# Out-projection order and low parts of the attention outputs in a two-layer hybrid encoder

## The chip, the cores and the metric

The kernel runs on one core of a Trainium2 chip. The metric is the device time of one execution in microseconds, as the median of several. An execution is a single launch that computes the whole output from the weights in HBM. The engines are named as the profile names them: PE is TensorE (matmuls), PEld its weight loads, DVE is VectorE, ACT ScalarE, POOL GpSimd, SP the engine that issues most DMAs.

## The reference, cut to what matters

A sequence of 512 tokens of width 1024 passes two layers. A layer is half a SwiGLU feed-forward block, a mixer, and another half block. The mixer projects the normalised input once and splits the columns among four groups of heads, each 256 wide:

```python
h = rms_norm(x, mix_norm)
aq, ak, av, bu, cq, ck, cv, dq, dk, dv = split(h @ w_in)
o_a = banded_attention(...)      # A: window +-128, sink, 4 query heads on 2 key heads
y_b = s5_bidirectional(bu, ...)  # B: state-space scan, then a half GLU
o_c = dilated_attention(...)     # C: three dilations, 4 heads
o_d = neighborhood_attention(...)# D: 2-D windows with a learned bias, 4 heads
x = x + concat([o_a, y_b, o_c, o_d]) @ w_out
```

All of it is in float32. The out-projection is a sum over the four groups, so its parts can be added to `x` in any order once the group is there.

## The kernel before

Activations lie transposed: `x` is eight tiles of 128 channels by 512 tokens. Every float32 product is made of three matmuls in a faster format: each operand is split into a rounded high part and the rest, the low part, and `mm3` (L107) multiplies the weights' low part with the activations' high part (L108), then high with low (L109), then high with high (L110). For the weights of layer 0's mixer ScalarE makes the high part (L126) and GpSimd the low one (L127); those of layer 1 were split ahead of time during layer 0's second feed-forward block, stored to DRAM, and are loaded as `wh` and `wl` by SP (L167, L168). There are four buffers for each of the two.

The mixer is a set of streams cut into steps, and the table `ORDER` (L35) says in which order the steps are written. `dq`, `dk`, `dv` and their like are projections. `Ds` is the first half of a step of D's attention (`first`, L736): scores, bias, exponentials, and GpSimd's division by the sum. `Dt` is the second (`second`, L769): transposing the probabilities, splitting them (L787 ScalarE high, L788 VectorE low) and multiplying by the values into `pot`. `A` and `C` are alike. Two heads share a tile `m` and then a split tile `mt` [128 x 2 x 512]: ScalarE copies half of `pot` to `tmp` (L796), VectorE adds the other half (L805, L801 for D), ScalarE writes the high part of `mt` (L808), and the low part follows on L809. S5 makes its own two `mt` (L958, L959). `mD`, `mB`, `mC` and `mA` are steps of the out-projection (`merge`, L814): D's pairs, S5's, C's two pairs together with A's first pair, and A's second pair. Each takes weights from `split`, sums in a bank of the tag `mm` (three banks), and VectorE adds the bank to `x` (L831).

The written order is a priority. A scheduler with its own estimate of durations orders each engine's instructions, so a step may be spread among others; at run time each engine goes through its list in order and waits on semaphores.

Of the kernel before, what the change touches and what calls it, by code (L numbers as in the profile page):

```python
# [15 lines left out]
ALU = mybir.AluOpType  # L16
# [18 lines left out]
ORDER = """  # L35
dq dq dq dk dk dq dq dk s5 dk dv cq dk s5 Ds dv dv ck cq ck Ds cq dv Ds dv Ds Ds s5 cq s5 Dt ck s5 Dt s5 Dt ck
cq s5 Ds cv Dt aq cv s5 aq Ds Dt Dt Ds ck Cs cv Dt s5 cv aq ak aq Cs s5 ak Dt Cs aq Cs Ct ak mD ak Cs Ct Cs Cs
Ct ak Cs Ct s5 mD Ct mD As Ct As Ct Ct As mD As As At As As mB At As At At At mC mC mB mB mC At At mC At mC mC
mC mB mC mA mA
"""  # L40
T2 = 15
# [30 lines left out]
def hybrid_encoder(ctx: ExitStack, tc: tile.TileContext, t: dict):  # L72
# [4 lines left out]
    tt = nc.vector.tensor_tensor  # L77
# [3 lines left out]
    gtt = nc.gpsimd.tensor_tensor  # L81
# [6 lines left out]
    def t2(name="t", dt=F32):  # L88
        return pool.tile([P, S], dt, tag="t2", bufs=T2, name=nm(name))

    def k4(shape, dt=F32, name="k"):
        return pool.tile(shape, dt, tag="k4", bufs=K4, name=nm(name))
# [7 lines left out]
    def bank(tag, name=None):  # L100
        bufs = {"mm": 3, "ot": 1, "sc": 2, "tp": 2}[tag]
        return ps.tile([P, 512], F32, tag=tag, bufs=bufs, name=nm("p" + (name or tag)))

    def f32(ap):
        return ap.bitcast(F32)
# [455 lines left out]
    def mixer(l, T, next_norm):  # L561
# [171 lines left out]
        def attention(res, qk, vs, band, biases, perm, is_a):  # L733
# [35 lines left out]
            def second(i, part):  # L769
                rows = slice(64 * (i % 2), 64 * (i % 2) + 64)  # L770
                vh = i % 2 if is_a else i
                v = vs[0]
                if part == 0:
                    live["ot"] = bank("ot", name="ot")
                pq = live[i]
                ot = live["ot"]
                order = (0, 3, 1, 2) if band else (0, 1, 2, 3)
                for kb in order[2 * part:2 * part + 2]:
                    qbs = [b for b in range(4) if pq[b][1] <= kb < pq[b][2]]
                    q0, q1 = qbs[0] * P, (qbs[-1] + 1) * P  # L780
                    n = q1 - q0
                    tp = bank("tp", name="tp")
                    for b in qbs:
                        c0 = (kb - pq[b][1]) * P
                        nc.tensor.transpose(tp[:, b * P - q0:(b + 1) * P - q0], pq[b][0][:, c0:c0 + P], ident)  # L785
                    pT = k4([P, 2, S], F32R, name="pT")
                    nc.scalar.copy(pT[:, 0, :n], tp[:, :n])  # L787
                    tt(pT[:, 1, :n], tp[:, :n], f32(pT[:, 0, :n]), op=ALU.subtract)  # L788
                    first = kb == 0
                    nc.tensor.matmul(ot[:, q0:q1], v[:, kb, vh, :], pT[:, 0, :n], start=first, stop=False)  # L790
                    nc.tensor.matmul(ot[:, q0:q1], v[:, kb, vh, :], pT[:, 1, :n], start=False, stop=kb == order[-1])  # L791
                if part == 0:
                    return
                live.pop(i)
                tmp = t2(name="tmp")
                nc.scalar.copy(tmp[0:64], ot[64:128])  # L796
                if i % 2 == 0:
                    live["m"] = t2(name="m")
                m = live["m"]
                if perm:  # L800
                    tt(m[rows].rearrange("p (r b c) -> p b r c", r=8, b=4),  # L801
                       ot[0:64].rearrange("p (b r c) -> p b r c", r=8, b=4),
                       tmp[0:64].rearrange("p (b r c) -> p b r c", r=8, b=4), op=ALU.add)
                else:
                    tt(m[rows], ot[0:64], tmp[0:64], op=ALU.add)  # L805
                if i % 2 == 1:
                    mt = k4([P, 2, S], F32R, name="mt")
                    nc.scalar.copy(mt[:, 0], m)  # L808
                    gtt(mt[:, 1], m, f32(mt[:, 0]), op=ALU.subtract)  # L809
                    res[i // 2].append(mt)  # L810

            return first, second
# [325 lines left out]
```

## Time and profile before

| | |
|---|---|
| median of three runs | 1983.24 us (1981.26 to 1988.75) |
| profiled execution | 1987.2 us, of it span 1985.4 |
| busy in the span | PE 1938.4, PEld 1634.4, DVE 1244.2, ACT 801.5, POOL 294.5 |
| mean granted clock of TensorE | 0.994 |

Times in the rows below are us from the start of the span. Layer 0's mixer ends near 640, layer 1's near 1635. A timeline row gives the start, the time that the instruction took, engine, line and tiles, and in brackets how long the engine was idle before it and what ended that. Matmuls overlap, so the distance between two starts is what one costs. A PEclk of 1.00 is 2.4 GHz, 0.50 is 1.2 GHz.

### The profile page before, as it was taken

The numbers are of one execution on the slowest core, as the hardware profiler recorded it, in microseconds if no ns is written. First come the engines' busy times: TensorE is split into PE (matmuls) and PEld (weight loads), VectorE is DVE, ScalarE is ACT, GpSimd is POOL, SyncE is SP. The second block draws the span as 40 slices with busy tenths as digits, with TensorE's granted clock in tenths as the row PEclk, the third lists the DMA queues.
The fourth block names the chain that finished last, engine by engine and source line by source line (L and its number), as shares of the span: only waits on it lengthen the run. The fifth ranks groups of instructions, "written<-read, shape, count | busy, mean of one in ns | idle before, by whom it ended". The sixth has DMA issues, their size and how long they took to land. (4 is left out here: it accounts for less than half of the span.)

```text
span 1985.4 us, 26849 instructions
## 1 busy us (share of the span) xinstructions
PE 1938.4 (98%) x9667; PEld 1634.4 (82%) x9667; DVE 1244.2 (63%) x2439; ACT 801.5 (40%) x1515; POOL 294.5 (15%) x403
## 2 busy tenths in 40 slices
PE   9999999999999999999999999899999999999999
PEld 7778878899977888888887888788998778888887
DVE  6976637748787554545677755475587865454454
ACT  5333323524675433333443333333346643232332
POOL 2121201112353010101022112000122310000000
PEclk9999999999999999999999999999999999999999
DMA  5444446564412362636455453544535223323233
GB/s 180 146 161 153 169 113 206 197 217 127 136 56 91 95 228 91 228 106 212 157 173 165 146 173 114 155 137 146 179 115 165 75 93 99 104 88 104 86 107 105
DMA packets 120229, 277.65 MB, mean 140 GB/s; under 512 B 24208, under 2 KB 33168, under 8 KB 120096
## 3 DMA queue, kind: packets, MB, share of 16 engines
q1 hardware_dynamic: 106496, 231.82, 38.3%
q0 software_dynamic: 13600, 44.12, 5.8%
q8 instruction: 76, 1.25, 0.3%
q14 instruction: 57, 0.47, 0.1%
HBM read 226.93 MB, written 48.99 MB: 139 GB/s over the span
## 5 line engine op out<-in xcount | busy, mean ns | idle before, releaser
L126 ACT CAST wh<-wr 128x512 fp32r<-128x512 f32 (+2 forms) x628 | 349.3, 564 | 758.8 <-PE pgp L110 264.8
L127 DVE TENSOR_TENSOR wl<-wr,wh 128x512 fp32r<-128x512 f32 (+2 forms) x610 | 390.7, 644 | 304.7 <-ACT wh L126 302.6
L108 PE MATMUL pop<-a,wl 128*128 128x512 f32 x704 | 275.3, 394 | 15.8 <-DVE wl L127 13.2
L108 PE MATMUL pgp<-hh,wl 128*128 128x512 f32 x704 | 274.3, 390 | 2.5 <-DVE wl L127 1.5
L108 PE MATMUL pup<-hh,wl 128*128 128x512 f32 x704 | 275.0, 391 | 0.4 <-DVE wl L127 0.4
L109 PE MATMUL pop<-a,wh 128*128 128x512 f32 x704 | 274.7, 390 | 0.0
L110 PE MATMUL pop<-a,wh 128*128 128x512 f32 x704 | 274.7, 390 | 0.0
L109 PE MATMUL pup<-hl,wh 128*128 128x512 f32 x704 | 274.5, 390 | 0.0
L109 PE MATMUL pgp<-hl,wh 128*128 128x512 f32 x704 | 274.2, 390 | 0.3 <-DVE hl L241 0.3
L110 PE MATMUL pup<-hh,wh 128*128 128x512 f32 x704 | 274.1, 389 | 0.0
L110 PE MATMUL pgp<-hh,wh 128*128 128x512 f32 x704 | 274.1, 389 | 0.0
L108 PEld LDWEIGHTS pop<-a,wl 128*128 128x128 f32 x704 | 132.5, 188 | 47.9 <-DVE wl L127 16.6
L108 PEld LDWEIGHTS pgp<-hh,wl 128*128 128x128 f32 x704 | 132.2, 188 | 31.3 <-DVE wl L127 2.3
L108 PEld LDWEIGHTS pup<-hh,wl 128*128 128x128 f32 x704 | 132.1, 188 | 28.7 <-DVE wl L127 0.8
L110 PEld LDWEIGHTS pop<-a,wh 128*128 128x128 f32 x704 | 132.5, 188 | 28.1
L109 PEld LDWEIGHTS pgp<-hl,wh 128*128 128x128 f32 x704 | 132.1, 188 | 27.9 <-DVE hl L241 0.6
L110 PEld LDWEIGHTS pup<-hh,wh 128*128 128x128 f32 x704 | 132.2, 188 | 27.5
L109 PEld LDWEIGHTS pup<-hl,wh 128*128 128x128 f32 x704 | 132.2, 188 | 27.4
L109 PEld LDWEIGHTS pop<-a,wh 128*128 128x128 f32 x704 | 132.6, 188 | 26.8
L110 PEld LDWEIGHTS pgp<-hh,wh 128*128 128x128 f32 x704 | 132.1, 188 | 27.3
L152 POOL DMA_DIRECT2D pd<-phi x86 | 47.0, 546 | 625.2 <-ACT phi L149 619.7
L108 PE MATMUL ppr<-wh,hl 128*128 128x256 f32 x448 | 129.5, 291 | 0.7 <-DMA wh<-pd 0.7
(275 smaller groups left out, 3054.3 us busy)
## 6 DMA issues: line engine op xcount, KB each, us to landing
wr<-in_f_w SPq DMA_DIRECT2D x172, 512.0 KB, 3.5
wr<-in_f_w SPq DMA_DIRECT2D x64, 384.0 KB, 3.3
wr<-in_f_w SPq DMA_DIRECT2D x64, 320.0 KB, 2.9
pd<-phi POOLq DMA_DIRECT2D x78, 256.0 KB, 3.9
pd<-plo POOLq DMA_DIRECT2D x78, 256.0 KB, 4.5
wl<-pd SPq DMA_DIRECT2D x78, 256.0 KB, 2.8
wh<-pd SPq DMA_DIRECT2D x78, 256.0 KB, 3.1
praw<-in_wm SPq DMA_DIRECT2D x68, 256.0 KB, 4.7
```

Of the source, the lines that this page charges most:

```text
L108: nc.tensor.matmul(out, ll, rh, start=start, stop=False)
L109: nc.tensor.matmul(out, lh, rl, start=False, stop=False)
L110: nc.tensor.matmul(out, lh, rh, start=False, stop=stop)
L126: nc.scalar.copy(hi[:, :w], r)
L127: (nc.gpsimd if pooled else nc.vector).tensor_tensor(lo[:, :w], r, f32(hi[:, :w]), op=ALU.subtract)
L152: nc.gpsimd.dma_start(dst[0], f32(hi[:, :step]))
```

## The change

Two edits. In the table one line differs (the new line is a permutation of the old): the first `mB` stands one A step later, the second and third stand ahead of the three `mC` that they followed, between A's steps; the last `mB` stays. And the low part of every attention `mt` is subtracted by VectorE (`tt`), not GpSimd (`gtt`).

```diff
-Ct ak Cs Ct s5 mD Ct mD As Ct As Ct Ct As mD As As At As As mB At As At At At mC mC mB mB mC At At mC At mC mC
+Ct ak Cs Ct s5 mD Ct mD As Ct As Ct Ct As mD As As At As As At mB As At At mB At mB mC mC mC At At mC At mC mC
 mC mB mC mA mA
...
                     nc.scalar.copy(mt[:, 0], m)
-                    gtt(mt[:, 1], m, f32(mt[:, 0]), op=ALU.subtract)
+                    tt(mt[:, 1], m, f32(mt[:, 0]), op=ALU.subtract)
```

L809 is issued twelve times, six in a layer. The scheduler orders anew what the table moves; both layers come out alike. Three places are shown, all of layer 0. In the names, `pop` are out-projection banks; their sources are `mt_5642` and `mt_5656` (S5), `mt_5628` and `mt_5826` (C's pairs), `mt_6056` (A's first pair) and `mt_6242` (A's second).

TensorE while A's heads begin, before: `ptp` are transposes of probabilities, `pot_5782` is C's last head, `p_5729` to `p_5771` belong to A's first head.

```order
L791 MATMUL pot_5782<-pT_5808,v_5084 128x512
L790 MATMUL pot_5782<-pT_5818,v_5084 128x512
L785 MATMUL ptp_5898<-ident,p_5729 128x128
L791 MATMUL pot_5782<-pT_5818,v_5084 128x512
L785 MATMUL ptp_5898<-ident,p_5735 128x128
L108 MATMUL pop_6142<-mt_5642,wl_6079 128x512
L109 MATMUL pop_6142<-mt_5642,wh_6078 128x512
L110 MATMUL pop_6142<-mt_5642,wh_6078 128x512
L108 MATMUL pop_6142<-mt_5656,wl_6079 128x512
L785 MATMUL ptp_5906<-ident,p_5765 128x128
L109 MATMUL pop_6142<-mt_5656,wh_6078 128x512
L110 MATMUL pop_6142<-mt_5656,wh_6078 128x512
```

The same transposes in the new order (`psc` are scores, 5833 to 5867 of A's second head, 5885 of its third):

```order
L790 MATMUL pot_5782<-pT_5808,v_5084 128x512
L791 MATMUL pot_5782<-pT_5808,v_5084 128x512
L785 MATMUL ptp_5898<-ident,p_5729 128x128
L790 MATMUL pot_5782<-pT_5818,v_5084 128x512
L785 MATMUL ptp_5898<-ident,p_5735 128x128
L791 MATMUL pot_5782<-pT_5818,v_5084 128x512
L785 MATMUL ptp_5906<-ident,p_5765 128x128
L785 MATMUL ptp_5906<-ident,p_5771 128x128
L749 MATMUL psc_5861<-o_5578,o_5304 128x384
L750 MATMUL psc_5861<-kl_5579,o_5304 128x384
L749 MATMUL psc_5867<-o_5578,o_5304 128x256
L750 MATMUL psc_5867<-kl_5579,o_5304 128x256
```

S5's products 6134 and 6142, which stood among these transposes, now stand further ahead. From `psc_5833` to the first product with `mt_6056` there are 24 out-projection matmuls in the old order and 9 in the new.

TensorE at the end of the mixer, before; `pot_6193` is A's last head, and after the last row ten more fillers follow up to the first product with `mt_6242`:

```order
L108 MATMUL pop_6298<-mt_5656,wl_6083 128x512
L109 MATMUL pop_6298<-mt_5656,wh_6082 128x512
L790 MATMUL pot_6193<-pT_6234,v_5441 128x384
L110 MATMUL pop_6298<-mt_5656,wh_6082 128x512
L791 MATMUL pot_6193<-pT_6234,v_5441 128x384
L108 MATMUL pop_6306<-mt_5642,wl_6083 128x512
L109 MATMUL pop_6306<-mt_5642,wh_6082 128x512
L110 MATMUL pop_6306<-mt_5642,wh_6082 128x512
L108 MATMUL pop_6306<-mt_5656,wl_6083 128x512
L109 MATMUL pop_6306<-mt_5656,wh_6082 128x512
```

The new order there:

```order
L109 MATMUL pop_6314<-mt_6056,wh_6251 128x512
L110 MATMUL pop_6314<-mt_6056,wh_6251 128x512
L790 MATMUL pot_6193<-pT_6225,v_5441 128x384
L791 MATMUL pot_6193<-pT_6225,v_5441 128x384
L790 MATMUL pot_6193<-pT_6234,v_5441 128x384
L791 MATMUL pot_6193<-pT_6234,v_5441 128x384
L108 MATMUL pop_6325<-mt_6242,wl_6280 128x512
L108 MATMUL pop_6335<-mt_6242,wl_6280 128x512
L108 MATMUL pop_6344<-mt_6242,wl_6280 128x512
```

In the old order fifteen matmuls stand between the last `pot_6193` and the first with `mt_6242`, in the new one none.

VectorE where S5's `mt` are split, before; `mb` are S5's unsplit outputs, `ISA` rows on L752 add the bias and take the minimum:

```order
L752 ISA p_5729,mn_5724<-psc_5726,bias_5722 128x256
L752 ISA mn_5724 128x1
L752 ISA p_5735,mn_5724<-psc_5732,bias_5722 128x384
L752 ISA mn_5724 128x1
L959 SCALAR_TENSOR_TENSOR mt_5642<-mb_5640,mt_5642 128x512
L959 SCALAR_TENSOR_TENSOR mt_5656<-mb_5654,mt_5656 128x512
L788 TENSOR_TENSOR pT_5681<-ptp_5676,pT_5681 128x512
```

And in the new order:

```order
L752 ISA p_5729,mn_5724<-psc_5726,bias_5722 128x256
L752 ISA mn_5724 128x1
L752 ISA p_5735,mn_5724<-psc_5732,bias_5722 128x384
L752 ISA mn_5724 128x1
L809 TENSOR_TENSOR mt_5628<-m_5517,mt_5628 128x512
L959 SCALAR_TENSOR_TENSOR mt_5642<-mb_5640,mt_5642 128x512
L959 SCALAR_TENSOR_TENSOR mt_5656<-mb_5654,mt_5656 128x512
L788 TENSOR_TENSOR pT_5681<-ptp_5676,pT_5681 128x512
```

The low part of C's first pair, which GpSimd subtracted, now stands in front of S5's two, and S5's products are summed into banks 71 to 73 in a row (71 and 72 before). On SP, layer 1 loads the second block of S5's weights ahead of C's first block; in the old order it was the other way round. GpSimd's list only loses L809 and has its weight subtractions in the new order of blocks.

## Rows read from the trace of the kernel before

**Rows 1.** The page, part 1: busy us (share of the span), instructions.

```profile
PE 1938.4 (98%) x9667; PEld 1634.4 (82%) x9667; DVE 1244.2 (63%) x2439; ACT 801.5 (40%) x1515; POOL 294.5 (15%) x403
```

**Rows 2.** Waits of TensorE, 560 to 640: us in total, times, longest.

```profile
PE pop L108 <- ACT mt L808: 1.8, 1, 1.8
PE pop L108 <- ACT mt L958: 1.5, 1, 1.5
```

**Rows 3.** Waits of TensorE, 1550 to 1625 (layer 1).

```profile
PE pop L109 <- DMA wh<-pd: 1.9, 1, 1.9
...
PE pop L108 <- ACT mt L958: 1.4, 1, 1.4
PE pop L108 <- DMA wl<-pd: 0.7, 1, 0.7
```

**Rows 4.** Timeline, 605 to 608, then layer 1: start, us, instruction [idle before].

```profile
605.25 0.42 PE L791 MATMUL pot<-pT,v 128*128 128x384 f32 x1
...
605.71 0.58 ACT L796 COPY tmp<-pot 64x512 f32<-64x512 f32 x1 [0.33 <-PE pot L791]
...
606.33 0.68 DVE L805 TENSOR_TENSOR m<-pot,tmp 64x512 f32<-64x512 f32 x1 [0.47 <-ACT tmp L796]
607.04 0.62 ACT L808 CAST mt<-m 128x512 fp32r<-128x512 f32 x1 [0.75 <-DVE m L805]
...
607.71 0.73 PE L108 MATMUL pop<-mt,wl 128*128 128x512 f32 x2 [1.82 <-ACT mt L808]
...
1592.09 1.64 PE L108 MATMUL pop<-mt,wl 128*128 128x512 f32 x3 [1.82 <-ACT mt L808]
```

**Rows 5.** Timeline at the end of the mixer, layer 0: TensorE, then ScalarE.

```profile
625.12 0.33 PE L791 MATMUL pot<-pT,v 128*128 128x384 f32 x1
625.29 0.40 PE L108 MATMUL pop<-mt,wl 128*128 128x512 f32 x1
...
628.74 0.61 PE L108 MATMUL pop<-mt,wl 128*128 128x512 f32 x2
...
627.41 0.62 ACT L808 CAST mt<-m 128x512 fp32r<-128x512 f32 x1
```

**Rows 6.** Groups by line and form: busy us, mean ns of one.

```profile
L788 DVE TENSOR_TENSOR pT<-ptp,pT 128x512 fp32r<-128x512 f32 x32 | 21.4, 681 | 4.7 <-ACT pT L787 4.6
...
L809 POOL TENSOR_TENSOR mt<-m,mt 128x512 fp32r<-128x512 f32 x12 | 15.4, 1287 | 39.7 <-ACT mt L808 39.7
```

**Rows 7.** Timeline near 575: TensorE, VectorE, GpSimd; VectorE in layer 1.

```profile
575.49 0.79 PE L109 MATMUL pop<-mt,wh 128*128 128x512 f32 x1 [0.20 <-POOL mt L809]
...
574.55 2.85 DVE L959 SCALAR_TENSOR_TENSOR mt<-mb,mt 128x512 fp32r<-128x512 f32 x2
...
574.16 1.28 POOL L809 TENSOR_TENSOR mt<-m,mt 128x512 fp32r<-128x512 f32 x1
...
1557.99 2.07 DVE L959 SCALAR_TENSOR_TENSOR mt<-mb,mt 128x512 fp32r<-128x512 f32 x2
```

**Rows 8.** Timeline of TensorE: nine matmuls from the first row to the second.

```profile
581.40 0.48 PE L108 MATMUL pop<-mt,wl 128*128 128x512 f32 x1
...
583.58 0.39 PE L790 MATMUL pot<-pT,v 128*128 128x512 f32 x1
```

**Rows 9.** Windows: length, busy us by engine (instructions), PEclk, DMA share, GB/s.

```profile
587.89:605.89 18.00, 17.30 (x98) 14.00 (x96) 14.70 (x48) 14.49 (x47) 9.51 (x15) 1.00 0.28 79
1574.20:1590.30 16.10, 14.41 (x82) 11.52 (x80) 12.00 (x43) 12.24 (x39) 6.37 (x11) 1.00 0.12 37
609.10:612.50 3.40, 3.40 (x13) 2.92 (x12) 1.74 (x4) 1.80 (x4) 0.81 (x2) 0.50 0.02 5
...
1600.50:1603.90 3.40, 3.40 (x15) 2.79 (x16) 0.69 (x1) 0.00 (x0) 0.00 (x0) 1.00 0.16 51
```

**Rows 10.** Timeline of the DMA issues on SP, layer 1.

```profile
1592.90 1.27 SPq L168 DMA_DIRECT2D wl<-pd  x3
1596.26 1.27 SPq L167 DMA_DIRECT2D wh<-pd  x3
```

## The prediction

> **What bounds the kernel now.** I read the page first: TensorE is busy for 1938.4 of 1985.4 us [rows 1], so time can only move where TensorE waits or runs at a lower clock. Then the waits of TensorE in the two mixer tails, which is where the change moves anything. In layer 0 there are two long ones: 1.5 us on S5's `mt` (call it wait 1) and 1.8 us on the `mt` of A's first pair (wait 2) [rows 2]. Layer 1 has the same two (1.4 us, and wait 2 again with 1.82 us) and two waits for weights, 1.9 and 0.7 us [rows 3, 4]. Everything else in the tails is dense. So even a perfect reordering could win only these, some 9 us, and what the clock loses behind them.
>
> Wait 2 is a fixed latency: the last `pot` matmul starts at 605.25 and ends at 605.67, ScalarE copies half of it, VectorE adds, ScalarE casts, and TensorE starts at 607.71 [rows 4]. From the end of that matmul to the first one that needs `mt` it is 2.04 us, whatever else happens. At the end of the mixer the same chain stands for A's second pair, but there TensorE has work: its last `pot` starts at 625.12, fifteen other matmuls follow from 625.29, and when TensorE comes to `mt` at 628.74 it has been ready since 628.03 [rows 5]. That covered chain and the stretch in front of wait 2 are what I look at in the change.
>
> **The change part by part.** All sums are against the profiled execution (1987.2 us, span 1985.4), which is 4.0 us above the median of 1983.24; I add the difference to the median.
>
> *Waits 1 and 2 themselves: 0.* In the new order the matmuls in front of both, and those that wait, stand at the same places; only which product is computed differs.
>
> *Low parts on VectorE, behind wait 1: +0.4 us a layer.* One such operation costs VectorE about 0.68 us (I take the `pT` subtraction, 681 ns, also 128x512) where GpSimd needed 1.287 [rows 6]. Where the low part of `mt` is waited for, that would be a gain of 0.6 us, but the trace has only one such wait on TensorE, 0.20 us at 575.49 [rows 7]. Behind wait 1 the new operation (C's first `mt`) is queued in front of the two L959 operations, whose results the very next TensorE matmuls now need; the C matmuls that stood between them are gone. L959 thus ends one operation later, TensorE waits about 0.6 instead of 0.2. Bounds 0 and 0.7; I take 0.4 more. The other low parts: those of D and of C's second pair have other matmuls between high and low part, and at wait 2 three L108 matmuls and a `pot` (0.8 us) cover 0.7. Nothing, at most one operation each.
>
> On L959 itself the trace shows 2.85 us for the two in layer 0, where GpSimd subtracts a low part beside them from 574.16, and 2.07 us in layer 1 [rows 7]. The Trainium skill says in "SBUF — State Buffer", Who interferes with whom, that a VectorE instruction with two SBUF inputs contends with a GpSimd instruction that reads SBUF; the trace agrees, 2.85 against 2.07. By that page the moved operation, which has two SBUF inputs itself, would be held up beside GpSimd as L959 was, this term would stand at its upper bound, 0.7 a layer, and the sum at +9.3.
>
> *S5 tokens earlier: +2.4 us a layer in front of wait 2.* In the old order 24 out-projection matmuls stand between the scores `psc_5833` of A's second head and wait 2, in the new one 9: fifteen S5 and C matmuls have moved ahead of that stretch. At 0.24 us each (nine from 581.40 to 583.58 take 2.18 [rows 8]) they are 3.6 us, of which I count 3.5, since the first after a transpose costs more. Ahead of the stretch there was no idle time for them to fill, so the stretch starts about 3.5 us later, and must end as early as before for the sum to be zero. Lower bound 0: A's work has slack. Upper bound 3.5: A's heads set the pace and every matmul taken away leaves a hole. Nearest row: in 18.0 us of this stretch in layer 0 VectorE is busy 14.7, ScalarE 14.5, and TensorE already idles 0.7 with the cover in place; in layer 1 it idles 1.7 of 16.1 [rows 9]. Taking away 3.5 leaves 14.5 us. VectorE has then three `x` additions less and one low part more (14.7 - 2 x 0.68 = 13.3), ScalarE about the same 14.5 less one weight cast. Engines that hand tiles to each other in order don't run at 95 to 100%, so I take 2.4, nearer the upper end.
>
> *The end of the mixer: +2.1 us a layer.* In the new order the last four `pot` matmuls stand behind all fillers, and the matmul after them is the first that needs A's second `mt`. The cover of fifteen matmuls is gone and wait 2's 2.04 us stands here too, call it wait 3. I count 2.0 to 2.7 (VectorE has a weight subtraction in front of the addition, 0.7) and take 2.1. This is the surest term, since it follows from the order of one engine.
>
> *Weights of layer 1: -1.1 us.* The wait of 0.7 on `wl` was for a block that is now loaded while S5's products run, so it goes. The one of 1.9 comes because three `wh` loads can't start until 1596.26, when the matmuls that hold the buffers are through, though the `wl` loads were issued at 1592.90 [rows 10]. Now those matmuls come two to three us sooner after wait 2, but TensorE also comes sooner to the block it needs: I take -0.4 (bounds -1.9 and +1).
>
> *Clock: 0.* Behind waits 1 and 2 the granted clock is at 0.5, the level of 1.2 GHz: 609.10 to 612.50 has 0.50 with TensorE busy throughout, so each such stretch costs up to 3.4/2 = 1.7 us. But the 1.9 us wait for `wh` left the clock at 1.00 [rows 9]. So a wait of this size may or may not cost 1.7. Of five, four did. With wait 3 there are two more chances, and the four old ones can fall either way: sum 0, bounds -6.8 and +3.4.
>
> The Trainium skill, in "TensorE: Matmul & The Clock Gate", What's actually happening, says that the gate is free-running and its effect "run-variable". The trace agrees: waits of 1.8 and 1.9 us ended differently. By that rule alone the four old losses might be absent in a new execution, which is the rival of the clock below.
>
> Sum: 2 x (0.4 + 2.4 + 2.1) - 1.1 + 0 = +8.7. Against the median: 1983.24 + 8.7 = 1992 us; the profiled execution would be near 1996.
>
> **Rivals.**
> 1. *Only wait 3.* A's heads have slack after all, the moved matmuls cost nothing in front of wait 2: 2 x 2.1 + 0.8 - 1.1 = +3.9, 1987. For it: VectorE and ScalarE each have a fifth of that stretch free. Against: TensorE idles there even with the cover.
> 2. *Slower beyond doubt.* A's heads set the pace fully (3.5 a layer) and wait 3 lowers the clock in both layers (1.7 each): 2 x (0.4 + 3.5 + 2.1 + 1.7) - 1.1 = +14.3, 1997.5. For it: wait 2, built the same, did so in both layers. Against: `wh` at 1.9 us did not. It decides from about 2.9 a layer in front of wait 2, or from one lowered clock more than before.
> 3. *Faster, by the clock.* The four stretches at half clock in the tails don't come: 4 x 1.7 = 6.8 less. With rival 1's small loss that is 3.9 - 6.8 = -2.9, 1980. For it: the clock spared the `wh` wait. Against: waits 1 and 2 stay as long as they are, and in both layers they lowered it. Even this doesn't reach half a per cent.
> 4. *Nothing happens.* The queues run as before and the moved work is the same work: 0, 1983. Against it wait 3, which follows from TensorE's own order.
>
> **How the numbers follow.** Half a per cent, 9.9 us, is about what a measurement of this kernel can tell from no change. Forecast 50% (its own range +5.5 to +12.5, the sizes of the two middle terms), rival 1 20%, rival 2 20%, rival 3 6%, rival 4 4%. The forecast lies just inside the bound: of its 50% some 24 are above +9.9, with all of rival 2 that makes slower 0.44; faster by half a per cent is left 0.03, for what I have not seen; the rest, 0.53, within. For 8 in 10 I leave out rivals 3 and 4 and the upper third of rival 2, 17% together: 1985 to 2000.
>
> **What would show it.** In the new trace: a wait on `mt` L808 of about 2 us at the last `pot` of each mixer, which is not there now; if it is absent, the forecast falls. From the scores `psc` of A's second head to wait 2 TensorE should idle 2 to 4 us in pieces below 1.5, on `pT` and on `mn`, where it idled 0.7 in layer 0; if less than 1, rival 1. Waits 1 and 2 should keep their 1.4 to 1.8 us; if either is gone, my reading of the order is wrong. The wait for `wl` in layer 1 should be gone and that for `wh` be 1 to 2 us. The low parts should show as VectorE operations of 0.6 to 0.7 us, longer beside GpSimd. The granted clock behind waits 1, 2 and 3 decides between forecast, rival 2 and rival 3.

## The result, and the profile after

The changed kernel takes 2000.68 us (median of eight runs, 1993.07 to 2003.67). The kernel before, run beside it and with the three runs shown earlier, has a median of 1987.78 over eight. The ratio is 1.0068, 95% interval 1.0050 to 1.0086: slower, by 12.9 us of medians. The forecast was 1992 with a range of 1985 to 2000, so the time lies just outside it, on the slow side. Two things, of nearly equal size, make up the 8.7 us between forecast and result: the median of before that I added to stood 4.5 us lower than that of more runs, and the change itself cost 4.2 us more than the sum of +8.7.

The profiled execution of the changed kernel took 2003.67 us (span 2001.9, mean granted clock 0.991). Its page, part 1, against [rows 1]:

```profile
PE 1946.6 (97%) x9667; PEld 1640.1 (82%) x9667; DVE 1251.2 (63%) x2451; ACT 801.9 (40%) x1515; POOL 278.2 (14%) x391
```

TensorE's count is the same and its busy time is 8.2 us longer, which, with the same instructions, fits more time at the lower clock. VectorE has the twelve low parts more, GpSimd twelve less. Waits of TensorE in layer 0, 560 to 650, against [rows 2] (total, times, longest):

```profile
PE pop L108 <- ACT mt L808: 4.0, 2, 2.3
PE pop L108 <- ACT mt L958: 1.6, 1, 1.6
PE psc L749 <- DVE mn L752: 1.4, 2, 1.2
PE pot L790 <- DVE m L805: 1.2, 1, 1.2
PE pop L109 <- DVE mt L959: 1.1, 1, 1.1
PE pot L791 <- DVE pT L788: 0.5, 1, 0.5
```

There are now two waits on L808: wait 2 is still there and wait 3 stands beside it. Four rows of 0.5 to 1.4 us follow, where before had nothing above 0.5. In layer 1, against [rows 3], the 0.7 on `wl` is gone and the wait for `wh` is 1.8:

```profile
PE pop L108 <- ACT mt L808: 3.7, 2, 2.1
...
PE pop L109 <- DMA wh<-pd: 1.8, 1, 1.8
```

The end of the mixer in layer 0, all engines (start, us, instruction, idle before), against [rows 5]:

```profile
634.24 0.33 PE L791 MATMUL pot<-pT,v 128*128 128x384 f32 x1
634.61 0.58 ACT L796 COPY tmp<-pot 64x512 f32<-64x512 f32 x1
634.62 0.69 DVE L127 TENSOR_TENSOR wl<-wr,wh 128x512 fp32r<-128x512 f32 x1
635.34 0.68 DVE L805 TENSOR_TENSOR m<-pot,tmp 64x512 f32<-64x512 f32 x1
636.06 0.62 ACT L808 CAST mt<-m 128x512 fp32r<-128x512 f32 x1 [0.87 <-DVE m L805]
...
636.82 1.07 PE L108 MATMUL pop<-mt,wl 128*128 128x512 f32 x2 [2.25 <-ACT mt L808]
```

This is wait 3, link by link: copy, a weight subtraction that stands in front of the addition, addition, cast. The fifteen matmuls that lay over it are gone, and TensorE is idle for 2.25 us.

In front of wait 2, TensorE, against [rows 4] and [rows 9]:

```profile
599.43 0.39 PE L749 MATMUL psc<-o,o 128*128 128x256 f32 x1 [1.17 <-DVE mn L752]
...
608.47 0.38 PE L790 MATMUL pot<-pT,v 128*128 128x256 f32 x1 [1.16 <-DVE m L805]
...
609.62 0.58 PE L791 MATMUL pot<-pT,v 128*128 128x256 f32 x1 [0.54 <-DVE pT L788]
...
615.05 0.97 PE L108 MATMUL pop<-mt,wl 128*128 128x512 f32 x3 [1.73 <-ACT mt L808]
```

Windows of the changed kernel (busy us by engine, then the granted clock): the 20.62 us up to the end of wait 2, then 3.4 us inside that stretch, behind wait 2, and behind wait 3:

```profile
594.43:615.05 20.62, 15.73 (x81) 12.19 (x80) 13.65 (x47) 14.10 (x43) 8.20 (x16) 0.92 0.20 62
609.40:612.80 3.40, 3.18 (x10) 2.44 (x11) 1.52 (x5) 1.38 (x6) 1.83 (x4) 0.54 0.45 135
615.20:618.60 3.40, 3.40 (x20) 2.99 (x21) 3.07 (x6) 2.39 (x7) 1.37 (x2) 1.00 0.02 5
636.90:640.30 3.40, 3.40 (x9) 2.62 (x10) 1.43 (x3) 0.36 (x1) 0.00 (x0) 0.51 0.31 125
```

The same length up to wait 2 in the kernel before:

```profile
587.09:607.71 20.62, 18.11 (x103) 14.69 (x101) 16.18 (x53) 16.33 (x50) 11.42 (x19) 1.00 0.28 83
```

TensorE's idle time in that window grew from 2.51 to 4.89 us. The clock, which in before fell behind wait 2, now falls behind the 1.16 and 0.54 us waits in front of it (0.54 from 609.40), is full behind wait 2 and falls again behind wait 3.

By number, though, these two executions don't differ in the tails: each has four stretches of 3.4 us at 0.50 there. The changed kernel's span has 12.9 us more at 0.50 in all (37.5 against 24.6), and they lie near 9, 1292 and 1415, in front of and between the tails, where the two kernels have the same instructions in the same order. A kernel that is no slower than before (e8, below) has such a stretch there too; the changed kernel, then e8:

```profile
1415.20:1422.00 6.80, 6.80 (x34) 6.80 (x34) 1.57 (x3) 0.00 (x0) 0.00 (x0) 0.50 0.55 189
1407.70:1414.53 6.83, 6.83 (x34) 6.83 (x34) 1.41 (x3) 0.00 (x0) 0.00 (x0) 0.50 0.57 207
```

So one profile of each kernel doesn't show what the change costs by the clock. That takes means over many executions, and a count over the profiles of all kernels, which stands with e13 to e16.

### The profile page after: what moved, and what is told of

Read it like the earlier page. It is cut to its first block, busy times and chain, and to the rows that moved or that the text cites. A ratio compares the mean times of both kernels' runs of the same rounds, so it can differ in the third digit from the quotient of the medians.

```text
span 2001.9 us, 26866 instructions
## 1 busy us (share of the span) xinstructions
PE 1946.6 (97%) x9667; PEld 1640.1 (82%) x9667; DVE 1251.2 (63%) x2451; ACT 801.9 (40%) x1515; POOL 278.2 (14%) x391
## 5 line engine op out<-in xcount | busy, mean ns | idle before, releaser
L108 PE MATMUL pop<-a,wl 128*128 128x512 f32 x704 | 275.9, 394 | 14.3 <-DVE wl L127 13.6
L110 PE MATMUL pop<-a,wh 128*128 128x512 f32 x704 | 275.3, 391 | 0.0
L109 PE MATMUL pop<-a,wh 128*128 128x512 f32 x704 | 275.3, 391 | 0.0
L109 PE MATMUL pgp<-hl,wh 128*128 128x512 f32 x704 | 274.7, 390 | 0.0
L109 PE MATMUL pup<-hl,wh 128*128 128x512 f32 x704 | 274.6, 390 | 0.0
L110 PE MATMUL pgp<-hh,wh 128*128 128x512 f32 x704 | 274.5, 390 | 0.0
L110 PE MATMUL pup<-hh,wh 128*128 128x512 f32 x704 | 274.1, 389 | 0.0
L110 PEld LDWEIGHTS pop<-a,wh 128*128 128x128 f32 x704 | 132.8, 189 | 28.0
L109 PEld LDWEIGHTS pgp<-hl,wh 128*128 128x128 f32 x704 | 132.5, 188 | 27.9 <-DVE hl L241 0.5
L109 PEld LDWEIGHTS pop<-a,wh 128*128 128x128 f32 x704 | 133.0, 189 | 27.2
L110 PEld LDWEIGHTS pgp<-hh,wh 128*128 128x128 f32 x704 | 132.5, 188 | 27.4
L109 PEld LDWEIGHTS pup<-hl,wh 128*128 128x128 f32 x704 | 132.2, 188 | 27.5
L110 PEld LDWEIGHTS pup<-hh,wh 128*128 128x128 f32 x704 | 132.2, 188 | 27.5
```

The costliest lines, as they stand in the source:

```text
L108: nc.tensor.matmul(out, ll, rh, start=start, stop=False)
L109: nc.tensor.matmul(out, lh, rl, start=False, stop=False)
L110: nc.tensor.matmul(out, lh, rh, start=False, stop=stop)
```

## The experiments

Each kernel was timed in turns with the kernel before on the same chip (before's medians in the four sessions: 1986.25, 1986.58, 1987.24, 1985.72). Each execution has its time and its mean granted clock. Their product is what I call the time at full clock, the rest is lost to the clock. This split is an estimate: it counts as lost also the half-clock time in which TensorE waits anyway. Both are means over a kernel's runs minus those of before in the same session (before: 1972.9 to 1974.2 at full clock, 11.9 to 14.1 lost). The standard error of a difference is 0.8 to 1.4 us at full clock and 0.9 to 1.9 us by the clock; the larger ones belong to the kernels with four to seven runs (e3, e5, e7 and e12 to e15; the others have ten to twelve).

| kernel | ratio, 95% interval | at full clock | by the clock |
|---|---|---|---|
| e1 tokens only | 1.0020, 1.0008 to 1.0033 | +3.9 | -0.2 |
| e2 all low parts only | 1.0046, 1.0031 to 1.0060 | +5.1 | +3.1 |
| e3 changed kernel | 1.0059, 1.0042 to 1.0076 | +6.7 | +5.2 |
| e4 later tokens, 39 of cover | 1.0022, 1.0009 to 1.0036 | +6.0 | -1.0 |
| e5 changed, cover kept | 1.0041, 1.0026 to 1.0057 | +4.5 | +4.5 |
| e6 A's first low part only | 1.0035, 1.0024 to 1.0046 | +5.1 | +2.4 |
| e7 changed, waits 2, 3 filled | 1.0072, 1.0052 to 1.0092 | +7.4 | +7.6 |
| e8 before, wait 2 filled | 1.0003, 0.9987 to 1.0020 | +1.1 | -0.2 |
| e9 new table, D's and A's last | 1.0019, 1.0003 to 1.0035 | +4.9 | -0.7 |
| e10 new table, C's | 1.0032, 1.0020 to 1.0044 | +5.2 | +1.3 |
| e11 old table, ten low parts | 0.9994, 0.9983 to 1.0005 | +1.2 | -2.1 |
| e12 tokens later still | 1.0059, 1.0043 to 1.0076 | +8.6 | +3.8 |
| e13 changed kernel | 1.0085, 1.0069 to 1.0102 | +6.9 | +9.6 |
| e14 as e13, C's on GpSimd | 1.0073, 1.0052 to 1.0095 | +9.1 | +5.1 |
| e15 as e13, A's first on GpSimd | 1.0052, 1.0036 to 1.0067 | +5.1 | +4.7 |
| e16 as e13, both on GpSimd | 1.0022, 1.0009 to 1.0035 | +3.8 | +0.7 |

### e1 and e2: one edit each; e3: both

The entries of the table are called tokens below. e1 has the new line of the table with `gtt` as before. e2 has the old table and:

```diff
-                    gtt(mt[:, 1], m, f32(mt[:, 0]), op=ALU.subtract)
+                    tt(mt[:, 1], m, f32(mt[:, 0]), op=ALU.subtract)
```

Expected of e1:

> Only the table's line is new; GpSimd still subtracts the low parts. In the order of this kernel TensorE has 9 out-projection matmuls in front of wait 2, as in the changed kernel, and keeps the cover of 15 matmuls at the end of the mixer, as before. Theory (both edits cost, and add up): the stretch in front of wait 2 is 2.6 us longer in layer 1 and up to 5.7 in layer 0, there is no wait 3, so +6 to +9 us against before, and about 4 us under the changed kernel. Rival 'wait 3 carries it': the stretch costs nothing, 0 to +2. Rival 'the tokens carry it all': +13, the same as the changed kernel.

Expected of e2:

> Only the twelve low parts are on VectorE; the table is the old one. The scheduler's new order has 18 out-projection matmuls among A's first transposes as before, but no cover at the end of the mixer: wait 3 should stand there with 2.0 to 2.3 us in both layers, and the stretch in front of wait 2 should be as before. Theory (both edits cost, and add up): +4 to +5 us, of which 4.2 are wait 3; with one or two lowered clocks behind wait 3 up to +8. Rival 'the tokens carry it all': within 1 us of before, since the clock behind wait 2 recovers what wait 3 costs. Rival 'wait 3 carries it': +13.

Expected of e3, the changed kernel again:

> The changed kernel again, as the measure on this chip for its two halves. +13 us (ratio 1.0065) if the first measurement holds; +8 to +9 if the first one was high by the course of its executions, as the profiled execution's 5 us outside the mixer tails suggest.

The tokens alone cost about 3.8 us, none of it by the clock, so my theory of +6 to +9 was too high there. The low parts alone cost 8.2, at the upper end of the +8 that I allowed for; 3.1 of it are the clock and 5.1 are time at full clock. Together they make 12, as much as the changed kernel (11.9 in e3). Both rivals fall: neither edit carries it all. In e1, TensorE in front of wait 2 and the window behind it:

```profile
597.29 0.38 PE L749 MATMUL psc<-o,o 128*128 128x256 f32 x1 [1.17 <-DVE mn L752]
...
605.43 0.39 PE L790 MATMUL pot<-pT,v 128*128 128x256 f32 x1 [0.42 <-DVE m L805]
...
606.59 0.39 PE L791 MATMUL pot<-pT,v 128*128 128x256 f32 x1 [0.47 <-DVE pT L788]
...
611.12 0.96 PE L108 MATMUL pop<-mt,wl 128*128 128x512 f32 x3 [1.82 <-ACT mt L808]
```

```profile
611.30:614.70 3.40, 3.40 (x21) 2.97 (x22) 2.10 (x5) 2.29 (x7) 1.49 (x2) 1.00 0.02 5
```

The thin front, nine out-projection matmuls in place of 24, leaves a wait of 1.17 on the scores' minimum, but the wait on L805 is 0.42 here, not 1.16, and behind a wait 2 of 1.82 us the clock is full. So an idle time of that length doesn't always lower it.

### e4 and e12: where the S5 steps stand

GpSimd keeps the low parts in both. The table's line, in e4 (the second and third `mB` later; the expectation below says first and third) and then in e12 (the first three `mB` behind the first two `mC`):

```diff
-Ct ak Cs Ct s5 mD Ct mD As Ct As Ct Ct As mD As As At As As mB At As At At At mC mC mB mB mC At At mC At mC mC
+Ct ak Cs Ct s5 mD Ct mD As Ct As Ct Ct As mD As As At As As mB At As At At At mC mC mC At At mB mC At mB mC mC
...
+Ct ak Cs Ct s5 mD Ct mD As Ct As Ct Ct As mD As As At As As At As At At At mC mC mB mB mC mB At At mC At mC mC
```

> GpSimd subtracts the low parts; a table with the first and third S5 step later, so that 39 matmuls stand between the last pot matmul and the first that needs A's second mt (15 before), and 9 in front of wait 2 as in the changed kernel. Theory: the cover at the end beyond some 9 matmuls (2.04 us) buys nothing, the thin front of wait 2 costs as in the kernel with the tokens alone: +6 to +9. Rival: matmuls that are not in front of wait 2 only move to the end, where TensorE is never without work, and the front costs nothing: 0 to +2.

> GpSimd subtracts the low parts; a table with S5's first step after the sixth step of A and the third later too, so that 6 out-projection matmuls are left among A's first transposes (18 before, 9 in the changed table), and 57 and 38 follow the last pot matmul at the end. Theory (TensorE has too little to do in front of wait 2): a longer sum of waits there than with 9, +5 to +8. Rival 'what isn't done there fills later gaps for nothing': 0 to +3.

e4 agrees in kind, though below the +6 to +9 expected (ratio 1.0022, about +4.4): cover beyond what wait 3 needs buys nothing, and the thin front costs as in e1. e12 is slower than its +5 to +8, at 1.0059 about +12, with longer waits in front of wait 2 in layer 0 (total, times, longest):

```profile
PE psc L749 <- DVE mn L752: 2.6, 2, 1.7
...
PE pot L790 <- DVE m L805: 1.2, 1, 1.2
PE pot L791 <- DVE pT L788: 0.9, 3, 0.5
PE ptp L785 <- DVE pT L788: 0.7, 1, 0.7
```

18, 9 and 6 matmuls among A's first transposes give 0, about +4 and +12 us (at full clock 0, +3.9 and +8.6), so that stretch has no slack to give.

### e5 and e6: wait 3 taken out, and put in alone

In the scheduler's order the cover of fifteen hangs on one operation a layer: the low part of A's first pair. On GpSimd the cover is there, on VectorE it isn't. e5 (new table) and e6 (old table):

```diff
-                    tt(mt[:, 1], m, f32(mt[:, 0]), op=ALU.subtract)
+                    (tt if not (is_a and i == 1) else gtt)(mt[:, 1], m, f32(mt[:, 0]), op=ALU.subtract)
...
-                    gtt(mt[:, 1], m, f32(mt[:, 0]), op=ALU.subtract)
+                    (tt if is_a and i == 1 else gtt)(mt[:, 1], m, f32(mt[:, 0]), op=ALU.subtract)
```

> The changed kernel, with one low part a layer back on GpSimd: that of A's first pair. With it the scheduler gives back the 15 matmuls of cover at the end of the mixer; the other ten low parts stay on VectorE and 9 matmuls stand in front of wait 2. The first runs gave +3.9 us of time at full clock for the tokens alone, +5.1 for the low parts alone, +7 for both, and a mean granted clock of 0.9937 before, 0.9938, 0.9922 and 0.991. Theory (the low parts cost by wait 3, 2.1 us a layer, and by the clock behind it): 4.2 us less idle time and a mean clock near 0.993 to 0.994, so +4 to +6 against before, the level of the tokens alone. Rival 'the ten other low parts cost, by loading VectorE in front of the chains that TensorE waits for': +9 to +12, as the changed kernel.

> The kernel before, with one low part a layer on VectorE, that of A's first pair (two operations in all). The scheduler's order then has no cover at the end of the mixer. Theory (wait 3 and its clock are what the low parts cost): wait 3 of 2.0 to 2.6 us in both layers, time at full clock +4 to +5, mean clock 0.992, +6 to +9 in all, like the kernel with all twelve. Rival 'the ten other low parts cost': +0 to +2. Rival 'the wait costs its own length alone': +4, mean clock 0.9937.

e6, TensorE at the end of the mixer and the window behind it:

```profile
630.96 0.33 PE L791 MATMUL pot<-pT,v 128*128 128x384 f32 x1
633.54 0.94 PE L108 MATMUL pop<-mt,wl 128*128 128x512 f32 x3 [2.25 <-ACT mt L808]
```

```profile
635.20:638.60 3.40, 3.40 (x10) 2.66 (x9) 2.77 (x5) 1.44 (x2) 0.00 (x0) 0.52 0.00 0
```

Two moved operations cost 7.5 us, within the +6 to +9 expected: 5.1 at full clock and 2.4 by the clock. That is wait 3 with its price. e5 went against the theory of +4 to +6: without wait 3 the changed kernel was still at 1.0041, some 8 to 9 us, nearer the rival's +9 to +12, and its clock did not recover. The ten other low parts cost something too, though with the old table (e11) they cost nothing.

### e7 and e8: work of no use inside the waits

```diff
                 nc.scalar.copy(tmp[0:64], ot[64:128])
+                keep = is_a and i % 2 == 1
+                if keep:
+                    dm = bank("tp", name="dm")
+                    for q in range(4):
+                        nc.tensor.transpose(dm[:, 64 * q:64 * q + 64], tmp[0:64, P * q:P * q + P], ident[0:64, 0:64])
...
+                if keep:
+                    for q in range(3):
+                        nc.tensor.transpose(dm[:, P * q:P * q + P], m[:, P * q:P * q + P], ident)
```

(e8: `keep = is_a and i == 1`, in the kernel before.)

> The changed kernel, with work of no use for TensorE inside waits 2 and 3 of both layers: four transposes of tmp (128x64 out) when ScalarE has copied it, three of m (128x128) when VectorE has added it, into a bank that nobody reads. The chain that ends in mt is not touched, so the products start when they did. Theory (idle time in these waits lowers the clock): the same time at full clock, but a mean granted clock of 0.993 to 0.994 in place of 0.991, so 4 to 6 us less than the changed kernel, +7 against before. Rival 'the clock falls in places that have nothing to do with these waits': mean clock 0.991, time as the changed kernel. Rival 'the transposes are in the way': more than the changed kernel.

> The kernel before, with the same transposes inside wait 2 of both layers (it has no wait 3). Theory: the half-clock stretch behind wait 2, up to 1.7 us where it comes, is gone: 1 to 3 us less than before, mean clock 0.9945 to 0.995. Rival 'the clock falls for other reasons': within 0.5 us of before, mean clock as before.

Both theories miss. e8 is as before (+0.9, with a standard error of 1.6), and e7 loses 7.6 us to the clock, no less than the changed kernel. In e7, TensorE in front of and inside wait 2 of layer 0, then two windows from 613.60 on:

```profile
613.53 0.55 PE L791 MATMUL pot<-pT,v 128*128 128x256 f32 x1 [0.54 <-DVE pT L788]
...
617.56 0.68 PE L801 MATMUL pdm<-ident,tmp 64*128 64x64 f32 x4 [0.67 <-ACT tmp L796]
...
618.66 0.84 PE L813 MATMUL pdm<-ident,m 128*128 128x128 f32 x3
```

```profile
613.60:617.00 3.40, 3.04 (x8) 1.86 (x8) 1.24 (x4) 1.17 (x5) 2.06 (x4) 0.50 0.46 135
617.00:620.40 3.40, 2.84 (x12) 2.53 (x13) 1.71 (x3) 1.50 (x3) 0.00 (x0) 0.50 0.00 0
```

The wait is filled as meant, and the clock stays at 0.50 through it, having fallen before it, behind the waits of 1.16 and 0.54. So in this execution too the clock is lost in the stretch with L805, and filling wait 2 could not help there. Behind the filled wait 3 of layer 0 the clock falls all the same (0.50 from 644.32 on). Why was not found out. The filling is made of transposes, and whether other matmuls in its place would have kept the clock up was not tested; so it isn't shown that idle time inside a wait is what lowers it.

### e9 to e11: whose low parts

New table in e9 and e10, old in e11; the condition for `tt`, with `gtt` otherwise (`perm` is true for D, `is_a` for A, `i` counts the heads):

```diff
+                    (tt if perm or (is_a and i == 3) else gtt)(mt[:, 1], m, f32(mt[:, 0]), op=ALU.subtract)
...
+                    (tt if not (is_a or perm) else gtt)(mt[:, 1], m, f32(mt[:, 0]), op=ALU.subtract)
...
+                    (tt if not (is_a and i == 1) else gtt)(mt[:, 1], m, f32(mt[:, 0]), op=ALU.subtract)
```

> The new table; on VectorE only the low parts of D's two pairs and of A's second, on GpSimd those of C's two pairs and of A's first (cover of 15 at the end kept). So far: tokens alone +3.9 us at full clock and none lost to the clock; the changed kernel with one low part back on GpSimd +4.6 at full clock and 4.4 lost to the clock, so wait 3 isn't what lowers the clock there. Theory (C's low parts do: they stand on VectorE in front of L959 and in front of A's L805 and lengthen two waits there to 1.1 us): L959 is waited for 0.3 us or less, L805 0.4, as with the tokens alone; +4, mean clock as before. Rival 'any low part on VectorE': +7 to +9, mean clock 0.003 below before.

> The complement: the new table, and on VectorE only the low parts of C's two pairs; D's and A's stay on GpSimd (cover of 15 kept). Theory (C's low parts lower the clock): waits of 0.6 to 1.1 us on L959 and of 1.16 on L805, half-clock stretches behind them, +8 to +9.5 with a mean clock of 0.002 to 0.003 below before. Rival 'any low part on VectorE': +5 to +6, since only four of ten are there. Rival 'the clock is a matter of the run': +4.

> The old table, all low parts on VectorE but that of A's first pair; the cover of 15 at the end and the 18 matmuls among A's first transposes are kept. It is what the kernel with all twelve has beyond the one with A's first pair alone (+7.8). Theory: with the thick cover C's low parts delay nothing that TensorE waits for, but L959: 0 to +2, mean clock as before to 0.001 below. Rival 'low parts on VectorE lower the clock whatever the order': +4.

e9 costs what the tokens alone cost, so the rival 'any low part on VectorE' falls. e10 is above it at 1.0032, about +6.5, below the theory's +8 to +9.5: it stands only 1.3 us down by the clock. e11 is as before, and its clock is no lower, so low parts on VectorE do not cost in every order. The wait on L805 in e9:

```profile
601.39 0.58 ACT L796 COPY tmp<-pot 64x512 f32<-64x512 f32 x1
...
602.75 0.39 PE L790 MATMUL pot<-pT,v 128*128 128x256 f32 x1 [0.43 <-DVE m L805]
```

and in e10:

```profile
601.44 0.61 ACT L754 ACTIVATE p<-p,mn 128x384 f32<-128x384 f32 x1
...
602.17 0.58 ACT L796 COPY tmp<-pot 64x512 f32<-64x512 f32 x1
...
603.52 0.39 PE L790 MATMUL pot<-pT,v 128*128 128x256 f32 x1 [1.16 <-DVE m L805]
```

The longer wait isn't VectorE being busy with one more operation. `ot` has one bank, so the next head's `pot` waits until L805 has read the last one, and L805 waits for ScalarE's copy. In e10's order ScalarE has another exponential (L754) in front of that copy, 0.61 us, and in TensorE's order six out-projection products (L109 and L110), which in e9 start at 596.99 between two groups of transposes, stand ahead of both.

### e13 to e16: two by two

The new table in all; `tt` for all (e13), for `perm or is_a` (e14), for `not (is_a and i == 1)` (e15), for `perm or (is_a and i == 3)` (e16).

> The changed kernel, for the two-by-two: wait 3 and C's low parts on VectorE. So far +11.8 to +13 against before, of it about 7 at full clock and 5 by the clock. All theories: the same here.

> The new table, the low parts of D and A on VectorE, those of C on GpSimd: wait 3 is there, the longer waits on L959 and L805 are not. Theory 'the clock goes with both, each by its share': +8 to +10, mean clock 0.001 to 0.0015 below before. Rival 'wait 3 alone lowers it': +11 to +13, as both. Rival 'C's low parts alone lower it': +6 to +8, mean clock as before, and time at full clock as both.

> The changed kernel with the low part of A's first pair on GpSimd: no wait 3, but C's low parts on VectorE. Theory 'both': +7 to +9, mean clock 0.001 to 0.0015 below before. Rival 'wait 3 alone': +4 to +6, mean clock as before (then the first run of this kernel, 0.0022 below before, was chance). Rival 'C alone': +9, mean clock 0.0025 below.

> The new table with D's and A's second low part on VectorE, C's and A's first on GpSimd: neither wait 3 nor the longer waits. All theories: +4 as before, mean clock within 0.0005 of before; the tokens' idle time alone.

By the clock: neither +0.7, C's low parts +4.7, wait 3 +5.1, both +9.6. Averaged over the two rows and columns, wait 3 brings 4.6 us and C's low parts 4.3, each with a standard error of 1.5, and they add up as far as these errors let one see. So the rivals in which one of them does it alone fall, e14's and e15's alike. At full clock: +3.8, +5.1, +9.1, +6.9, so wait 3 costs 5.4 without C's low parts and 1.8 with them (each with an error of about 1.8), 3.6 on average. All three kernels with one or both were dearer than forecast: e13 by medians 17.0 against +11.8 to +13, e14 14.3 against +8 to +10 (its rival had +11 to +13), e15 10.6 against +7 to +9. The median of the kernel before is lower beside these four than beside the others (1985.72), which may be part of it. The changed kernel itself lost 5.2 us by the clock in e3 and 9.6 in e13, so the size is known no better than that. Windows of 3.4 us of e14, ahead of and behind its wait 2 in layer 0 and behind its wait 3:

```profile
605.30:608.70 3.40, 2.15 (x12) 1.36 (x11) 1.56 (x5) 1.56 (x5) 2.06 (x4) 1.00 0.46 135
609.80:613.20 3.40, 3.40 (x21) 2.95 (x21) 3.02 (x7) 2.37 (x7) 1.42 (x2) 1.00 0.02 5
631.70:635.10 3.40, 3.40 (x9) 2.66 (x10) 1.43 (x3) 0.43 (x1) 0.00 (x0) 0.50 0.32 130
```

and of e15 ahead of its wait 2 in layer 1, behind the waits on L805 and `pT`:

```profile
1600.20:1603.60 3.40, 2.18 (x7) 1.06 (x5) 1.42 (x3) 1.28 (x3) 2.06 (x4) 0.50 0.00 0
```

With wait 3 the clock is lost behind it; with C's low parts it is lost ahead of wait 2, where e14 kept it.

A count over all eighteen profiles bears this out. In eight (the changed kernel, e3, e5, e7, e10, e12, e13, e15) TensorE waits 1.15 us or more on L805 in both layers, and in all 16 places the clock falls to 0.50 between that wait and 1.5 us behind wait 2. In the ten others, where the wait on L805 is 0.94 us or less, it does so in 5 of 20 places, and in none of the eight of e1, e9, e14 and e16, which have the new table. e12 has the longer wait without any low part on VectorE, and it lost 3.8 us by the clock; so the fall goes with the waits in that stretch and not with the engine of the low parts. By the mean e10 fits less well, with the longer wait and only 1.3 us lost. Behind wait 3 it falls in all seven places of layer 0 (2.25 to 2.60 us, and filled in e7) and in two of seven of layer 1 (2.11 us); at the same place without wait 3, never.

## Why the prediction was wrong, point by point

**The step of the sum that failed is "Clock: 0".** I let two more chances for a lower clock and four old ones that may fall either way cancel. They don't: as a mean over runs the changed kernel loses 5.2 (e3) to 9.6 us (e13) more to the clock than before. By the two-by-two about half comes with wait 3, which I had listed only as a chance (2.4 us where it stands alone, e6). The other half comes with C's low parts, by the longer waits on L805 in front of wait 2 and on L959, which I had down as 0.4 us a layer and as pieces without a price by the clock. Not every added wait costs: with the tokens alone, 1.17 us on the scores' minimum and 0.42 on L805, nothing is lost (e1, e9, e16). Rival 2 had wait 3's part, with 1.7 a layer, and nothing for the others; the 3.5 us a layer that it put in front of wait 2 did not come.

**The base failed too.** I added the sum to the median of three runs, 1983.24, although the profiled execution stood 4.0 us above it. With more runs the median of before is 1985.7 to 1987.8. That alone moved the forecast by 2.5 to 4.5 us. With 1987.78 and the same sum it would have been 1996.5, and a range moved with it would have held the result; the miss in the sum would then have stood behind a time that looked right.

**Wait 3, +2.1 a layer: right in place and size.** 2.25 us in layer 0 (the weight subtraction stood in front of the addition, as allowed for in 2.0 to 2.7) and 2.11 in layer 1. Measured by itself it is 5.1 us at full clock (e6), against 4.2 in the sum. The cause wasn't the table, as the prediction's wording by "the new order" leaves open: the table alone keeps the cover (e1), and the low part of A's first pair on VectorE alone takes it away (e6), through the scheduler.

**S5's tokens, +2.4 a layer less 1.1 for the weights: right as a sum, in part by luck.** 2 x 2.4 - 1.1 = +3.7; the tokens alone cost 3.3 to 4.5 us by medians and means (e1, and e9 and e16 with six harmless low parts besides). In e1's profile the one term is smaller and the other larger than I had them: in the 20.62 us up to wait 2 of layer 0 TensorE idles 4.48 us, 1.97 more than before, and the two waits for weights in layer 1 shrink by 2.0 us. Rival 1, by which they cost nothing, falls. The window of e1:

```profile
590.50:611.12 20.62, 16.14 (x91) 12.73 (x90) 14.35 (x50) 15.57 (x48) 9.52 (x17) 1.00 0.22 64
```

In the changed kernel the idle time from the scores to wait 2 came in pieces of the size named: 1.17, 1.16 and 0.54, 2.87 us in all. The piece on L805 belongs to the other edit, though; with the tokens alone it is 0.42.

**Low parts behind wait 1, +0.4 a layer: right in kind, too small in layer 0.** TensorE waits 1.09 us on L959 in layer 0, where it waited 0.20 on L809 before [rows 7]: 0.9 more, above the upper bound of 0.7. In layer 1 it is 0.30. TensorE, VectorE and GpSimd in layer 0:

```profile
578.24 0.50 PE L109 MATMUL pop<-mt,wh 128*128 128x512 f32 x1 [1.09 <-DVE mt L959]
...
576.11 1.47 DVE L809 TENSOR_TENSOR mt<-m,mt 128x512 fp32r<-128x512 f32 x1
577.50 1.28 DVE L959 SCALAR_TENSOR_TENSOR mt<-mb,mt 128x512 fp32r<-128x512 f32 x2
...
575.75 1.28 POOL L127 TENSOR_TENSOR wl<-wr,wh 128x512 fp32r<-128x512 f32 x1
```

The moved operation took 1.47 us beside GpSimd's weight subtraction, and 0.69 as the median of the twelve. The rule of the Trainium skill in "SBUF — State Buffer", Who interferes with whom, by which the term would stand at its upper bound of 0.7, bears on layer 0, and the trace agrees, 1.47 against 0.69. In layer 1 GpSimd is idle beside the operation, which takes 0.69. The prediction read the price of this from 2.85 against 2.07 us for the two L959, which is too little: in layer 1 of before GpSimd's subtraction, from 1557.64 to 1558.92, still stood beside the first of them. Alone the two take 1.28 us, as above.

**Weights of layer 1, -1.1: open.** The wait on `wl` went, as said; that on `wh` shrank by 0.1, not 0.4, in this profile. In the profiles of e3 and e13, which are the same kernel, there is no wait on `wh` above 0.2 us, so one execution doesn't settle this term.

**Waits 1 and 2** stayed, 1.59 and 1.73 in layer 0, 1.84 and 1.61 in layer 1.

At full clock the parts are 6.7 to 6.9 us (e3, e13) against the 8.7 of my sum, which had no clock in it. So the sum without the clock was good to 2 us; what it left out was 5 us or more.

What stays open: whether C's low parts alone with the new table (e10, 1.3 us by the clock) really lose less than with D's and A's beside them (e5 and e15, 4.5 to 4.7), since the errors of these are 1.3 to 1.6; why filled waits (e7) lose no less; and what in these stretches lowers the clock.

## What to carry to other kernels

Price a wait that is added to a dense TensorE at its length plus what the clock takes behind it: here, 2.1 us of wait 3 a layer came to 3.7 us (e6, 7.5 in two layers). Whether a lowered clock comes after a single wait of 1.8 us could not be told from one execution here, but a zero mean was the wrong guess for added waits: behind the lengthened wait on L805 it came every time. Take the base from as many runs as the result will have. And moving one small operation to another engine can reorder a scheduled kernel elsewhere: look in the order for what it covered before, and put only those operations back that cost the cover (ten of twelve moved with the old table cost nothing).

## What the runs showed of the hardware

In the profiles the isolated stretches at 0.50 in the mixer tails last 3.4 us, so each costs up to 1.7 us where TensorE is busy throughout, and kernels differ in how many there are: four in the profile of before and of the changed kernel, one in e1, six in e5 and e6 (a stretch of double length counted as two). The same kind of wait is followed by 0.50 in one execution and 1.00 in the next (wait 2 in before and in e1). The stretch in front of wait 2 had 1.00 in e14 and 0.50 in e15, where C's low parts were on VectorE, and the count of 16 in 16 places against 5 in 20 says that this is more than chance. The Trainium skill's "run-variable" ("TensorE: Matmul & The Clock Gate", What's actually happening) is borne out for a single execution; the mean over runs, however, fell by 0.0025 (e3) to 0.005 (e13) with the change.

A 128x512 subtraction on VectorE with both inputs in SBUF took 0.69 us by itself and 1.47 beside a GpSimd subtraction of 1.28 us (the changed kernel at 599.70 and 576.11).
